# A two-block transformer layer on one core: expert rows fetched one pair ahead, weight buffers split seven and nine, the residual's squares summed later

## The chip, the core and the metric

One NeuronCore of a Trainium2 chip runs the whole program in one launch. Five engines work side by side, each with its own instruction queue: TensorE (PE in the profile; its weight loads are PEld), VectorE (DVE), ScalarE (ACT), GpSimd (POOL) and SyncE (SP, which here only issues transfers). The metric is the device time of one execution in microseconds (us); lower is better.

## The reference

The input is 512 tokens of width 2048, in float32. The first block is a mixer (half convolution, half a recurrent scan) with a residual, `h = x + mixed @ w_out`, followed by a mixture of experts: `v = rms_norm(h)`, a router picks a group of 8 experts by the group logits, then the best 2 of the group for every token, and

    hid = silu(xblk @ w_gate[e]) * (xblk @ w_up[e]);  h += gate * (hid @ w_down[e])

for 32 experts with `w_gate`, `w_up` of 2048 x 512 and `w_down` of 512 x 2048. A last RMS norm gives x1. The second block norms x1 again, makes attention, a state-space branch and two gates from projections of it, merges them, and returns `x1 + merged @ w_out`. The two norms in a row need, per token, the sum of the squares of h (for x1 itself, the residual) and a weighted sum of the same squares (for the input of the second block).

## The kernel before, in words

The program has three phases on one instruction stream per engine. A scheduler orders each engine's instructions when the kernel is built, by program order and by the time at which it thinks the operands are ready; on the chip each engine then runs its queue in that order. `issue_after(x)` only tells the scheduler to put the instructions of a block behind x on x's engine.

**Phase A** (lines 168 to 659) is the mixer. Its end is `w_out(1, held)` (lines 250 to 279): for four column blocks of 512 it multiplies, adds the residual, writes the rows of h to a DRAM tensor `dTok` (line 274, POOL's queue), and calls `routed` (lines 703 to 740), which transposes the block into `hT`, adds to the router's logits and sums squares for the first norm. For the first three blocks the logits are made with the 36 router columns as the stationary operand (line 721) and turned at the end (line 729), for the last with tokens as the stationary operand (line 735).

**Phase B** (lines 743 to 1013) is the mixture of experts, worked in 16 pairs of experts; each expert of a pair has 64 rows (slots). Weights come in loads of 1 MiB (line 676, SP's queue), 24 for a pair: 8 gate, 8 up, 8 down. They go round 16 buffers of 8 KB per partition, in two pools: `NW[0]` = 11 on the right side of the SBUF, which exist while phase A still runs and are filled during `w_out(1)` (line 260), and `NW[1]` = 5 on the left, which take over memory of phase A and are filled at the start of phase B (line 993). `slot` (line 685) deals the buffers out in turn; the 8 down loads of the last pair use left buffers only, since the right side is given to the next phase's activations (`last`, line 980).

For a pair p these steps follow one another:

- `first` (line 801) makes a one-hot matrix `oh` from the ranks (line 780, DVE), multiplies it with token numbers, scale and gate (line 784, PE), turns the result into row numbers (line 790, DVE) and fetches the rows of h from `dTok` into the one buffer `xg` by an indirect transfer on POOL's queue (line 791).
- `turned` (line 808) transposes `xg` in 16 matmuls (line 815, PE), scales it (line 816) into the one buffer `xT`, and transposes `oh` (line 820).
- `main` (line 907) multiplies `xT` with gate and up weights (line 916), makes `hid` (lines 921 to 929), multiplies it with the down weights (line 937), and adds the result, spread over the tokens by lines 946 and 947, to `hT` (line 948).

In program order `first` of pair p+1 stands ahead of `main` of pair p, and `turned` of pair p+1 stands inside it, behind the last up matmul (`then`, line 918). After pair 7 (`BREAK`) the order is interrupted: 15 weight loads are put ahead (line 1007), a branch looks whether any expert has more than 64 tokens (`overflow`, line 955), and only then `first` and `turned` of pair 8 follow, with nothing of a pair beside them. Before the first fetch `xg` is filled with zeros (line 768, POOL), so that slots without a token hold finite numbers.

**Phase C** (lines 1188 to 1464) is the second block. At its start 16 squares are made from `hT` (line 1212, ACT), and two sums over them are kept at once: `acc[1]`, weighted, on DVE (line 1215), and `acc[0]`, plain, on POOL (line 1216). Each ends in a matmul with ones and a reciprocal square root (lines 1219 to 1223): R for the projections, R1 for the residual, which is used in the very last stage only (line 1460). Beside this the dense projections begin: each load of weights is rounded by ACT (line 47), the rest is taken by DVE (line 48), and three matmuls per step use them (lines 111 to 113). hT is written to the DRAM tensor `dX` (line 1230). Much later comes the gated stage (lines 1429 to 1439), two dense products per step with two activation functions.

Of the kernel before, what the change touches and what calls it, by code (L numbers as in the profile page):

```python
# [15 lines left out]
NW = (11, 5)  # L16
# [82 lines left out]
def weights(k, src, kts, m, key="w", eng=None):  # L99

    nc = k.nc
    raw = k.wraw.tile([128, kts, m], F32, name=key + "raw")
    k.wload = nc.sync.dma_start(raw, src)
    wh = k.wspl.tile([128, kts, m], F32R, name=key + "h")
    wl = k.wspl.tile([128, kts, m], F32R, name=key + "l")
    split(nc, raw, wh, wl, eng)
    return wh, wl

# [59 lines left out]
def phase_a(k):  # L168
# [81 lines left out]
    def w_out(half, held=None):  # L250

        mh, ml = mix[half]
        for i, n in enumerate((3, 0, 1, 2) if half else range(4)):
            ns = slice(n * 512, (n + 1) * 512)
            ps = held if half and n == 3 else [k.psd.tile([128, T], F32, name="pd") for _ in range(4)]
            for j in range(8):
                wh, wl = weights(k, a["w_out"][half, n, j], 1, 512, eng=None if half else nc.gpsimd)
                if half and (j == 7 or i and j % 2):
                    with tc.issue_after(k.wload.ins):
                        k.ahead(1, NW[0])  # L260
                for t in range(4):
                    ts = slice(t * 128, (t + 1) * 128)
                    mm3(nc, ps[t], mh[:, j, ts], ml[:, j, ts], wh[:, 0], wl[:, 0], j == 0 and ps is not held,
                        j == 7 and (half == 1 or n < 3))
# [382 lines left out]
    k.dH = tc.dram_tile([T, D], F32, name="dTok")  # L647
    k.rw = rm.tile([128, KT, 36], F32, name="rw")
    k.lgT = tmp.tile([128, T], F32, name="sg")
# [53 lines left out]
def routed(k, psr, tmp, xs, n, i):  # L703

# [10 lines left out]
    if i < 3:  # L718
        pl = psr.tile([128, T], F32, name="pr")
        for j in range(4):  # L720
            nc.tensor.matmul(pl[0:36], k.rw[:, 4 * n + j], k.hT[:, 4 * n + j], start=j == 0, stop=j == 3)
        if i == 0:
            nc.scalar.activation(k.lgT[0:36], pl[0:36], AF.Copy)
        else:
            nc.vector.tensor_add(k.lgT[0:36], k.lgT[0:36], pl[0:36])
        if i == 2:
            pl = psr.tile([128, 4, 36], F32, name="pr")
            for t in range(4):
                nc.tensor.transpose(pl[:, t], k.lgT[0:36, t * 128:(t + 1) * 128], k.ident[0:36, 0:36])
            nc.scalar.activation(k.lg, pl, AF.Copy)  # L730
    else:
        pl = psr.tile([128, 4, 36], F32, name="pr")
        for t in range(4):
            for j in range(4):
                nc.tensor.matmul(pl[:, t], k.hT[:, 4 * n + j, t * 128:(t + 1) * 128], k.rw[:, 4 * n + j],
                                 start=j == 0, stop=j == 3)
        nc.vector.tensor_add(k.lg, k.lg, pl)
# [5 lines left out]
def phase_b(k, upto):  # L743
# [24 lines left out]
    nc.gpsimd.memset(xg, 0.0)  # L768
# [138 lines left out]
    def main(xT, info, oht, es, load=k.take, then=None, last=None):  # L907
        nq = slice(0, 64 * len(es))
        pgu = [ps0.tile([128, 512], F32, name=n) for n in ("pgate", "pup")]
        for j0 in range(0, KT, 4):  # L910
            for wi, which in enumerate(("gate", "up")):
                ws = [load(e, which, j0 // 4) for e in es]
                for j in range(4):
                    for i, w in enumerate(ws):
                        q = slice(i * 64, (i + 1) * 64)
                        nc.tensor.matmul(pgu[wi][q], xT[:, j0 + j, q], w[:, j * 512:(j + 1) * 512],  # L916
                                         start=j0 + j == 0, stop=j0 + j == KT - 1)
        if then is not None:
            then()
# [60 lines left out]
    def last():  # L980

        k.bctx.close()
        k.uctx = ExitStack()
        up = k.uctx.enter_context(tc.tile_pool(name="u2", bufs=1, side=RIGHT))
# [8 lines left out]
    k.ahead(NW[1])  # L993
    fr = {}
    prep(0)
# [3 lines left out]

    for p in range(16):  # L1000
        soon = p < 15 and p != BREAK
        if soon:
            ahead_of(p + 1)
        main(*fr.pop(p), (2 * p, 2 * p + 1), k.take, (lambda: prep(p + 1)) if soon else None,
             last if p == 15 and upto != "b" else None)
        if p == BREAK:
# [3 lines left out]
            prep(p + 1)  # L1010
# [177 lines left out]
def phase_c(k, out):  # L1188
    nc, tc, a = k.nc, k.tc, k.a
    ctx = ExitStack()  # L1190
    k.wraw = ctx.enter_context(tc.tile_pool(name="wraw2", bufs=4, side=LEFT))
# [8 lines left out]
    R = c.tile([128, T], F32, name="R")  # L1200

# [6 lines left out]
    with tc.tile_pool(name="nrm", bufs=2, side=LEFT) as np_:  # L1208
        acc = [np_.tile([128, T], F32, name="acc%d" % i, bufs=1) for i in range(2)]
        for f in range(KT):  # L1210
            sq = np_.tile([128, T], F32, name="nsq", bufs=4) if f else acc[0]
            nc.scalar.activation(sq, k.hT[:, f], AF.Square)
            g = col(k, "gg", f)
            if f:
                nc.vector.scalar_tensor_tensor(acc[1], sq, g, acc[1], op0=OP.mult, op1=OP.add)
                nc.gpsimd.tensor_add(acc[0], acc[0], sq)
            else:
                nc.vector.tensor_scalar(acc[1], sq, g, None, op0=OP.mult)
        for x, r, e in ((acc[1], R, 1e-12), (acc[0], R1, 1e-6)):
            pr = psr.tile([128, T], F32, name="pr")  # L1220
            nc.tensor.matmul(pr, k.ones, x, start=True, stop=True)
            nc.vector.tensor_scalar(x, pr, 1.0 / D, e, op0=OP.mult, op1=OP.add)
            rsqrt(k, tmp, x, [128, T], r)
# [202 lines left out]

    yp = ctx2.enter_context(tc.tile_pool(name="ysp", bufs=1, side=RIGHT))
# [13 lines left out]

    wp = ctx2.enter_context(tc.tile_pool(name="mg2", bufs=1, side=LEFT))
# [135 lines left out]
```

## Time and profile before

| what | value |
|---|---|
| median of 3 runs | 3401.13 us (3394.83 to 3404.06) |
| the profiled execution's own time | 3402.26 us |
| its span, first to last instruction | 3400.6 us |
| mean granted TensorE clock | 0.963 of full speed |
| busy: PE, PEld, DVE, ACT, POOL | 93%, 63%, 49%, 31%, 16% |
| share of the chain that ended last | PE 46%, DMA 4%, POOL 2%, DVE 1% |

Times inside the execution are counted from the first instruction. Phase B's expert pairs take from about 1032 to 2041 us. In the rows further down, `out<-in` are the kernel's names, x is a count, a number in brackets is the idle time of the engine just before the row, with what ended it, and a name with two forms of a matmul's size (128*64) gives rows and columns of the array that it uses.

### The profile page before, as it was taken

Reading aid. Unit: us, or ns where it says so; the run is one execution under the profiler, and the core shown is the slowest. Engines: PE = TensorE matmul, PEld = TensorE weight load, DVE = VectorE, ACT = ScalarE, POOL = GpSimd, SP = SyncE. Lnnn points to the kernel's source line nnn. Section 1 sums busy time; section 2 is a strip of 40 time slices with the busy share of each in tenths; the row PEclk is TensorE's granted clock in tenths of the full one; section 3 lists DMA queues with packets and bytes.
Section 4 is the critical chain, followed back from the end, with each engine's and each line's share of the span. In section 5 each row is a group of like instructions: output and inputs, shape, how many; then the busy total and the mean of one; then the engine's idle time right before and its main releaser. Section 6 shows DMA issues by size and latency. Waiting matters only on the chain.

```text
span 3400.6 us, 41331 instructions
## 1 busy us (share of the span) xinstructions
PE 3171.8 (93%) x15156; PEld 2156.7 (63%) x15157; DVE 1658.1 (49%) x3072; ACT 1052.2 (31%) x1793; POOL 546.0 (16%) x581
## 2 busy tenths in 40 slices
PE   8999998779989899898999898999999999999999
PEld 6777666547664333333333346778777878888887
DVE  6666667993332222232223238445799443344433
ACT  6464564344330000000000024363322242353322
POOL 3052254543210000000000005372000100000000
PEclk9999999789999999899999998999999999999999
DMA  4445444767668999998999965435332653334343
GB/s 149 129 122 139 125 121 123 139 131 181 219 239 352 420 420 414 406 407 349 419 420 411 404 249 167 143 144 166 134 106 104 203 183 118 124 130 137 133 146 118
DMA packets 352495, 743.47 MB, mean 219 GB/s; under 512 B 110688, under 2 KB 176608, under 8 KB 302112
## 3 DMA queue, kind: packets, MB, share of 16 engines
q1 hardware_dynamic: 272576, 650.24, 52.1%
q10 hardware_dynamic: 70624, 60.52, 7.2%
q0 software_dynamic: 9088, 30.03, 2.7%
q8 instruction: 121, 1.98, 0.2%
q14 instruction: 86, 0.70, 0.1%
HBM read 674.96 MB, written 73.01 MB: 220 GB/s over the span
## 4 chain that ended last, share of the span: by engine, by line
PE 46%; DMA 4%; POOL 2%; DVE 1%; issue 1%; ACT 0%; ACTq 0%; SPq 0%; DVEq 0%; POOLq 0%
PE pd L113 10%; PE pd L111 10%; PE pd L112 10%; PE pgate L916 3%; PE py L937 3%; PE pup L916 2%; DMA xg<-dTok,ix 1%; DMA w<-expert_w_gate_dram 1%; PE pb L946 1%; PE pb L947 1%; PE pb L815 1%; PE pr L1345 1%; POOL cn L1115 1%; PE ps L1296 0%; POOL cm L1114 0%
## 5 line engine op out<-in xcount | busy, mean ns | idle before, releaser
L48 DVE TENSOR_TENSOR wl<-wraw,wh 128x512 fp32r<-128x512 f32 x636 | 478.0, 754 | 496.0 <-ACT wh L47 487.1
L47 ACT ACTIVATE wh<-wraw 128x512 fp32r<-128x512 f32 x668 | 418.0, 628 | 834.0 <-PE pd L112 677.7
L113 PE MATMUL pd<-u2h,wl 128*128 128x512 f32 x1088 | 437.7, 402 | 10.2 <-DVE wl L48 10.1
L111 PE MATMUL pd<-u2h,wh 128*128 128x512 f32 x1088 | 439.4, 404 | 6.4 <-ACT wh L47 6.4
L112 PE MATMUL pd<-u2l,wh 128*128 128x512 f32 x1088 | 436.6, 401 | 0.0
L113 PE MATMUL pd<-uh,wl 128*128 128x512 f32 x688 | 282.6, 411 | 42.8 <-DVE wl L48 42.8
L916 PE MATMUL pgate<-w,xT 128*64 128x512 f32 x1024 | 305.6, 615 | 15.7 <-DMA w<-expert_w_gate_dram 15.0
L916 PE MATMUL pup<-w,xT 128*64 128x512 f32 x1024 | 293.5, 595 | 0.0
L111 PE MATMUL pd<-uh,wh 128*128 128x512 f32 x688 | 278.7, 406 | 12.0 <-ACT uh L220 7.2
L112 PE MATMUL pd<-ul,wh 128*128 128x512 f32 x688 | 278.1, 404 | 5.0 <-DVE ul L221 5.0
L113 PEld LDWEIGHTS pd<-u2h,wl 128*128 128x128 f32 x1088 | 206.5, 190 | 63.7 <-DVE wl L48 14.0
L309 POOL TENSOR_TENSOR cv<-cv,tap 128x512 f32<-128x512 f32 x150 | 227.6, 1517 | 105.1 <-ACT tap L308 92.4
L111 PEld LDWEIGHTS pd<-u2h,wh 128*128 128x128 f32 x1088 | 206.9, 190 | 56.7 <-ACT wh L47 9.0
L937 PE MATMUL py<-w,hidT 128*64 128x512 f32 x1024 | 236.0, 599 | 2.9 <-ACT hidT L929 2.9
L112 PEld LDWEIGHTS pd<-u2l,wh 128*128 128x128 f32 x1088 | 206.9, 190 | 47.8 <-issue 1.1
L948 DVE TENSOR_TENSOR hT<-hT,pb 128x512 f32<-128x512 f32 x256 | 159.2, 681 | 148.9 <-PE pb L947 148.9
L941 DVE SCALAR_TENSOR_TENSOR yl<-py,info,yh 128x512 fp32r<-128x512 f32 x64 | 48.0, 750 | 311.1 <-ACT yh L940 311.1
L916 PEld LDWEIGHTS pgate<-w,xT 128*64 128x64 f32 x1024 | 87.5, 142 | 170.0 <-issue 157.4
L113 PEld LDWEIGHTS pd<-uh,wl 128*128 128x128 f32 x688 | 134.0, 195 | 82.8 <-DVE wl L48 53.7
L916 PEld LDWEIGHTS pup<-w,xT 128*64 128x64 f32 x1024 | 87.0, 137 | 135.8 <-issue 133.6
L791 POOL DMA_INDIRECT xg<-dTok,ix x16 | 16.1, 1007 | 918.7 <-DVE info L798 908.3
L937 PEld LDWEIGHTS py<-w,hidT 128*64 128x64 f32 x1024 | 71.9, 137 | 143.8 <-issue 133.9
(566 smaller groups left out, 5054.8 us busy)
## 6 DMA issues: line engine op xcount, KB each, us to landing
w<-expert_w_gate_dram SPq DMA_DIRECT2D x128, 1024.0 KB, 14.7
w<-expert_w_up_dram SPq DMA_DIRECT2D x128, 1024.0 KB, 16.0
w<-expert_w_down_dram SPq DMA_DIRECT2D x128, 1024.0 KB, 14.0
wraw<-w_out_dram SPq DMA_DIRECT2D x128, 256.0 KB, 2.7
wraw<-w_rkv_dram SPq DMA_DIRECT2D x96, 256.0 KB, 3.0
wraw<-w_conv_dram SPq DMA_DIRECT2D x64, 256.0 KB, 3.5
wraw<-w_ga_dram SPq DMA_DIRECT2D x64, 256.0 KB, 2.6
wraw<-w_gs_dram SPq DMA_DIRECT2D x64, 256.0 KB, 2.6
```

The lines of the kernel that those rows point to most:

```text
L47: nc.scalar.activation(h, x, AF.Copy)
L48: (eng or nc.vector).tensor_sub(l, x, h)
L111: nc.tensor.matmul(ps, ah, bh, start=first, stop=False)
L112: nc.tensor.matmul(ps, ah, bl, start=False, stop=False)
L113: nc.tensor.matmul(ps, al, bh, start=False, stop=last)
L309: nc.gpsimd.tensor_add(cv[p], cv[p], pr)
L815: nc.tensor.transpose(ps[:, j, 0:m], xg[0:m, (j0 + j) * 128:(j0 + j + 1) * 128], k.ident[0:m, 0:m])
L916: nc.tensor.matmul(pgu[wi][q], xT[:, j0 + j, q], w[:, j * 512:(j + 1) * 512], start=j0 + j == 0, stop=j0 + j == KT - 1)
L937: nc.tensor.matmul(py[q], hidT[:, j, q], w[:, j * 512:(j + 1) * 512], start=j == 0, stop=j == 3)
L941: nc.vector.scalar_tensor_tensor(yl[nq], py[nq], info[nq, 0:1], yh[nq], op0=OP.mult, op1=OP.subtract)
L946: nc.tensor.matmul(ps, yh[nq, fs], og, start=True, stop=False)
L948: nc.vector.tensor_add(hT[:, f], hT[:, f], ps)
```

## The change

- `NW` becomes (7, 9). In `w_out(1)` fewer expert loads are put ahead: one in the first column block and two in each of the others, seven in all.
- `routed` makes the logits of all four blocks with tokens as the stationary operand.
- `xg` is filled by a transfer of 128 rows of x on POOL's queue in place of the zeros.
- In `main`, what `then` holds is ordered behind the last up matmul on PE. It now holds `turned` of pair p+1 and then `first` of pair p+2, so that the rows of pair p+2 are fetched as soon as the transposes of pair p+1 have read `xg`. At the break pair 8 is fetched and turned as before, then pair 9 fetched.
- At the start of phase C only the weighted sum is made. The plain sum moves behind the gated stage: 16 tiles of `dX` are loaded back on ACT's queue, squared by ACT and added by POOL, then normed to R1.
- Some tiles without use (`pad`, `fill`, an early `xr`) move addresses and hold no instruction.

```diff
-NW = (11, 5)
+NW = (7, 9)
...
+def pad(k, ctx, side, n):
+
+    p = ctx.enter_context(k.tc.tile_pool(name="pad", bufs=1, side=side))
+    return p.tile([128, n // 4], F32, name="pad")
...
-                if half and (j == 7 or i and j % 2):
+                if half and (j == 7 or i and j == 3):
                     with tc.issue_after(k.wload.ins):
                         k.ahead(1, NW[0])
...
+    rm.tile([128, 512], F32, name="xr", bufs=4)
     k.rw = rm.tile([128, KT, 36], F32, name="rw")
-    k.lgT = tmp.tile([128, T], F32, name="sg")
...
-    if i < 3:
-        pl = psr.tile([128, T], F32, name="pr")
+    pl = psr.tile([128, 4, 36], F32, name="pr")
+    for t in range(4):
         for j in range(4):
-            nc.tensor.matmul(pl[0:36], k.rw[:, 4 * n + j], k.hT[:, 4 * n + j], start=j == 0, stop=j == 3)
...
+            nc.tensor.matmul(pl[:, t], k.hT[:, 4 * n + j, t * 128:(t + 1) * 128], k.rw[:, 4 * n + j], start=j == 0,
+                             stop=j == 3)
+    if i:
+        nc.vector.tensor_add(k.lg, k.lg, pl)
     else:
...
+        nc.vector.tensor_copy(k.lg, pl)
...
-    nc.gpsimd.memset(xg, 0.0)
+    nc.gpsimd.dma_start(xg, a["x"][0:128])
...
-                        nc.tensor.matmul(pgu[wi][q], xT[:, j0 + j, q], w[:, j * 512:(j + 1) * 512],
+                        up = nc.tensor.matmul(pgu[wi][q], xT[:, j0 + j, q], w[:, j * 512:(j + 1) * 512],
                                          start=j0 + j == 0, stop=j0 + j == KT - 1)
         if then is not None:
-            then()
+            with tc.issue_after(up.ins):
+                then()
...
+        pad(k, k.uctx, RIGHT, 480)
...
-    k.ahead(NW[1])
-    fr = {}
-    prep(0)
...
+    def prepare(p):
+
+        prep(p)
+        if p < 15 and p != BREAK:
+            ahead_of(p + 1)
+
+    k.ahead(NW[1])
+    fr = {}
+    prepare(0)
     for p in range(16):
-        soon = p < 15 and p != BREAK
-        if soon:
-            ahead_of(p + 1)
-        main(*fr.pop(p), (2 * p, 2 * p + 1), k.take, (lambda: prep(p + 1)) if soon else None,
+        main(*fr.pop(p), (2 * p, 2 * p + 1), k.take, (lambda: prepare(p + 1)) if p < 15 and p != BREAK else None,
              last if p == 15 and upto != "b" else None)
         if p == BREAK:
             k.ahead(sum(NW), sum(NW) - 1)
             overflow()
             ahead_of(p + 1)
-            prep(p + 1)
+            prepare(p + 1)
...
+    pad(k, ctx, LEFT, 128)
...
+    c.tile([128, 48], F32, name="fill")
...
-        acc = [np_.tile([128, T], F32, name="acc%d" % i, bufs=1) for i in range(2)]
+    with tc.tile_pool(name="nrm", bufs=1, side=LEFT) as np_:
+        acc = np_.tile([128, T], F32, name="acc")
         for f in range(KT):
...
-                nc.vector.scalar_tensor_tensor(acc[1], sq, g, acc[1], op0=OP.mult, op1=OP.add)
-                nc.gpsimd.tensor_add(acc[0], acc[0], sq)
+                nc.vector.scalar_tensor_tensor(acc, sq, g, acc, op0=OP.mult, op1=OP.add)
...
+        token_norm(acc, R, 1e-12)
...
+    pad(k, ctx2, RIGHT, 480)
...
     gctx.close()
 
+    with tc.tile_pool(name="nr1", bufs=2, side=RIGHT) as np_:
+        acc = np_.tile([128, T], F32, name="acc", bufs=1)
+        for f in range(KT):
+            x = np_.tile([128, T], F32, name="x")
+            nc.scalar.dma_start(x, k.dX[f])
+            if f:
+                nc.scalar.activation(x, x, AF.Square)
+                nc.gpsimd.tensor_add(acc, acc, x)
+            else:
+                nc.scalar.activation(acc, x, AF.Square)
+        token_norm(acc, R1, 1e-6)
```

`token_norm` is the body of the old loop over the two sums: a matmul with ones, a scale on DVE and `rsqrt`.

## Rows read from the trace of the kernel before

**Rows 1.** The page's 40 slices of the span (85 us each), GB/s of transfers.

```profile
GB/s 149 129 122 139 125 121 123 139 131 181 219 239 352 420 420 414 406 407 349 419 420 411 404 249 167 143 144 166 134 106 104 203 183 118 124 130 137 133 146 118
```

**Rows 2.** Windows: length, busy PE, PEld, DVE, ACT, POOL (count), clock, DMA share, GB/s.

```profile
983.00:1009.00 26.00, 26.00 (x131) 19.36 (x129) 7.38 (x11) 6.08 (x15) 2.16 (x4) 1.00 0.17 59
1009.00:1036.00 27.00, 12.71 (x69) 9.65 (x69) 13.96 (x52) 3.47 (x5) 4.00 (x3) 0.62 0.55 214
1051.00:1311.00 260.00, 238.91 (x1072) 97.09 (x1068) 69.45 (x117) 18.99 (x29) 3.98 (x4) 0.96 1.01 420
1532.00:1558.00 26.00, 19.68 (x92) 10.71 (x94) 4.22 (x11) 0.60 (x1) 1.99 (x2) 0.77 0.52 197
2041.00:2078.00 37.00, 26.02 (x84) 19.51 (x85) 36.32 (x35) 14.94 (x25) 22.50 (x14) 0.72 0.14 50
2960.00:3048.00 88.00, 88.00 (x386) 72.19 (x386) 39.11 (x57) 53.49 (x71) 0.00 (x0) 1.00 0.38 128
```

**Rows 3.** The tile xg: waits for its fetches (us, times), their time to landing.

```profile
  DMA xg<-dTok,ix: 66.0, 12
...
DMA to landing us min/median/max: 5.0/9.1/10.0
```

**Rows 4.** Timeline of PE in the expert stage: start us, us, instruction, [idle before].

```profile
1188.95 4.41 PE L916 MATMUL pgate<-w,xT 128*64 128x512 f32 x12 [1.36 <-DMA w<-expert_w_gate_dram]
...
1431.30 1.06 PE L784 MATMUL pb<-G,oh 128*128 128x6 f32 x8
...
1442.98 3.65 PE L815 MATMUL pb<-ident,xg 128*128 128x128 f32 x16 [7.06 <-DMA xg<-dTok,ix]
...
1447.41 1.90 PE L916 MATMUL pgate<-w,xT 128*64 128x512 f32 x6
...
1525.33 0.40 PE L947 MATMUL pb<-oht,yl 128*128 128x512 f32 x1
...
1539.76 3.65 PE L815 MATMUL pb<-ident,xg 128*128 128x128 f32 x16 [6.29 <-DMA xg<-dTok,ix]
...
1544.04 3.65 PE L916 MATMUL pgate<-w,xT 128*64 128x512 f32 x14
...
1638.51 3.22 PE L916 MATMUL pgate<-w,xT 128*64 128x512 f32 x13 [1.36 <-DMA w<-expert_w_gate_dram]
...
1699.60 5.08 PE L916 MATMUL pgate<-w,xT 128*64 128x512 f32 x12 [0.68 <-DMA w<-expert_w_gate_dram]
...
1959.99 2.47 PE L916 MATMUL pgate<-w,xT 128*64 128x512 f32 x10
```

**Rows 5.** DMA queues from 1040 to 1500 us: packets, MB, share.

```profile
q0 software_dynamic: 1008, 3.85, 2.1%
```

**Rows 6.** Timeline of SP: the first refills of the expert stage.

```profile
1035.64 12.62 SPq L676 DMA_DIRECT2D w<-expert_w_down_dram  x8
```

**Rows 7.** Timeline of DVE around the start of phase C.

```profile
2033.63 2.07 DVE L990 SCALAR_TENSOR_TENSOR u2l<-hT,vec,u2h 128x512 fp32r<-128x512 f32 x3
...
2042.76 1.77 DVE L1215 SCALAR_TENSOR_TENSOR acc<-nsq,vec,acc 128x512 f32<-128x512 f32 x1
...
2045.05 2.83 DVE L990 SCALAR_TENSOR_TENSOR u2l<-hT,vec,u2h 128x512 fp32r<-128x512 f32 x2
```

**Rows 8.** Timeline of PE at the start of phase C.

```profile
2050.45 0.80 PE L113 MATMUL pd<-u2h,wl 128*128 128x512 f32 x1 [6.44 <-DVE wl L48]
...
2070.26 0.79 PE L113 MATMUL pd<-u2h,wl 128*128 128x512 f32 x1 [2.40 <-DVE wl L48]
```

**Rows 9.** Groups by line, 985 to 1010 us: busy us, mean ns.

```profile
L735 PE MATMUL pr<-rw,hT 128*128 128x36 f32 x32 | 3.7, 276 | 0.0
...
L721 PE MATMUL pr<-hT,rw 128*36 128x512 f32 x8 | 3.6, 596 | 0.0
```

**Rows 10.** DMA issues: KB each, median us to landing.

```profile
xr<-x_dram ACTq DMA_DIRECT2D x16, 256.0 KB, 4.9
...
us<-dX ACTq DMA_DIRECT2D x16, 256.0 KB, 2.7
```

More of the change, by code (lines that the diff above doesn't have):

```diff
@@ L717, in routed @@
             nc.scalar.activation(ht, pt, AF.Copy)
-    if i < 3:
-        pl = psr.tile([128, T], F32, name="pr")
+    pl = psr.tile([128, 4, 36], F32, name="pr")
+    for t in range(4):
         for j in range(4):
-            nc.tensor.matmul(pl[0:36], k.rw[:, 4 * n + j], k.hT[:, 4 * n + j], start=j == 0, stop=j == 3)
[L722 to L730, printed above, removed]
-    else:
[L732 to L737, printed above, removed]
+            nc.tensor.matmul(pl[:, t], k.hT[:, 4 * n + j, t * 128:(t + 1) * 128], k.rw[:, 4 * n + j], start=j == 0,
+                             stop=j == 3)
+    if i:
+        nc.vector.tensor_add(k.lg, k.lg, pl)
+    else:
+        nc.vector.tensor_copy(k.lg, pl)
     for t, x in enumerate(xs):
@@ L1206, in phase_c, with token_norm @@
     u = k.u
-    with tc.tile_pool(name="nrm", bufs=2, side=LEFT) as np_:
-        acc = [np_.tile([128, T], F32, name="acc%d" % i, bufs=1) for i in range(2)]
+    def token_norm(x, r, e):
+        pr = psr.tile([128, T], F32, name="pr")
+        nc.tensor.matmul(pr, k.ones, x, start=True, stop=True)
+        nc.vector.tensor_scalar(x, pr, 1.0 / D, e, op0=OP.mult, op1=OP.add)
+        rsqrt(k, tmp, x, [128, T], r)
+    with tc.tile_pool(name="nrm", bufs=1, side=LEFT) as np_:
+        acc = np_.tile([128, T], F32, name="acc")
         for f in range(KT):
-            sq = np_.tile([128, T], F32, name="nsq", bufs=4) if f else acc[0]
+            sq = np_.tile([128, T], F32, name="nsq", bufs=4)
             nc.scalar.activation(sq, k.hT[:, f], AF.Square)
@@ L1214, in phase_c @@
             if f:
-                nc.vector.scalar_tensor_tensor(acc[1], sq, g, acc[1], op0=OP.mult, op1=OP.add)
-                nc.gpsimd.tensor_add(acc[0], acc[0], sq)
-            else:
[L1218 to L1223, printed above, removed]
+                nc.vector.scalar_tensor_tensor(acc, sq, g, acc, op0=OP.mult, op1=OP.add)
+            else:
+                nc.vector.tensor_scalar(acc, sq, g, None, op0=OP.mult)
+        token_norm(acc, R, 1e-12)
     for i in range(8):
```

## The prediction

> **What bounds the kernel now.** The page's slices come first: in ten of the 40 the transfers run at 404 to 420 GB/s, nowhere else above 352 [rows 1]. That is the expert stage, and the windows inside it say the same: 420 GB/s and a full DMA share over 260 us [rows 2]. A pair needs 24 loads of 1 MiB, 25.17 MB, and its gather, 0.55 MB (3.85 MB on POOL's queue for the seven gathers of 1040 to 1500 us [rows 5]); at 420 GB/s that is 61.2 us. The trace shows that pace where PE waits for weights: two gate matmuls released by a landing weight, of pair 10 and pair 11, start at 1638.51 and 1699.60, 61.1 us apart [rows 4].
>
> The tile xg shows the second limit: 12 times the transposes waited for the gather, 66.0 us in all, and a gather takes 9.1 us to land in the median [rows 3]. The timeline shows why: pair 7's rows are asked for by line 784, which ends at 1432.36, and PE has 3.6 us of pair 6's up matmuls left before it stands at 1435.92, so 7.06 us of the flight lie open [rows 4]. While PE stands, the 16 buffers fill and the transfers pause later. PE then starts a pair later than its weights allow, and each pair adds to that lag. At the two places where pairs cannot overlap, the break and the end, the lag turns into time.
>
> At the start of phase C the windows row from 2041 to 2078 tells another story: DVE 36.32 of 37 us, PE only 84 matmuls at a granted clock of 0.72 (a mix of the levels 1.2 and 2.4 GHz) [rows 2]. The gated stage gives 386 matmuls in 88 us, 0.228 us each, with PE never idle; 84 of them are 19.2 us, so 17.8 of the 37 us are lost.
>
> **The change part by part.** A measurement of this kernel can tell about 0.3%, 10 us, from no change.
>
> *Gather ahead, up to the break.* The wait of 7 us goes; the next thing late is the weights. I count from a matmul that waited for its weights: pair 3's at 1188.95. Four pairs at 61.2 us later, pair 7 could begin at 1433.8; it began at 1447.41 [rows 4]. Gain 13.6 us.
>
> *The same, behind the break.* Pair 11's gate waited for its weights at 1699.60; four pairs later is 1944.4, and pair 15 began at 1959.99 [rows 4]. Gain 15.6 us. PE can keep that pace: the saturated 260 us moved 109 MB, 4.25 pairs, and PE was busy 238.91 us of them, 56 us a pair [rows 2].
>
> *The break itself.* From the last matmul of pair 7 (1525.33) to the first of pair 8 (1544.04) nothing is taken out: branch, one-hot, gather, transposes stay in line. The open gather waited 6.29 us there while the transfers were idle [rows 2, 4]; with PE earlier, the 15 loads put ahead are still in flight, and the gather lands in 9.1 us [rows 3]. Loss 2.8 us (from 0 to 3.7, the longest landing being 10.0). The hole of the transfers here, 197 GB/s over 26 us [rows 2], stays: they wait for pair 8's first matmuls, which move as a whole.
>
> *Seven and nine buffers, the fill of xg.* Four loads, 4.2 MB or 10 us at 420 GB/s, move from `w_out(1)` to the start of phase B, and xg's fill adds 1 MiB, 2.5 us. From 1009 us on that makes nine loads, the fill and a gather: 11.0 MB, 26 us, done at 1035, while the first refill is only issued at 1035.64 [rows 6]; the stretch had 214 GB/s, the one before 59 [rows 2]. So the bytes cost nothing, but pair 0's gather, which landed in 5.0 us, the shortest, now shares the engines: 9.1 us, a loss of 4.1 (from 0, if left buffers are free before 1009 us, to 7, if it lands behind everything) [rows 3]. On POOL's queue the fill stands ahead of the norm's power (line 164), which it can hold up by about an issue; POOL's three instructions of that stretch took 4.00 us, 1.3 each [rows 2], so 0 to 1.3, and I take 0, since the fill waits for the last rows' writes and the power for the last logits, which end at about the same time. In the last pair nine left buffers instead of five hold the eight down loads. PE did not wait for those; but it would at the new pace, so this guards the 15.6 us and adds nothing. SP's queue gets no new order beyond this.
>
> *Order on PE.* Line 784 of the pair after next stands behind the transposes. Behind it wait `hid`'s transposes, one microsecond later, which is its duration [rows 4], at a point where PE is ahead of its weights: 0, bounds -1 and 1 us per pair.
>
> *Router.* 32 narrow matmuls take 3.7 us, the 8 wide ones 3.6 [rows 9]; three blocks change: 0.
>
> *Phase C's start.* POOL's 15 adds go. Beside them a DVE add took 1.77 us and two u2l 2.83 us; without them three u2l took 2.07, 0.69 each [rows 7]. Ahead of the first late weight rest that is (1.77 - 0.69) + (2.83 - 1.38) = 2.5 us of PE's wait of 6.44. The second wait, 2.40 [rows 8], stands behind slow adds alone and goes; of the 9.0 us that remain of the 17.8, lost to the lower clock behind the waits above all, I take a third, 3.0. Gain 7.9 us, from 2.4 to 17.8. The Trainium skill (GPSIMD Engine Reference, section 1, Specifications) says that POOL shares its SBUF interfaces with VectorE, with contention for VectorE instructions that have two SBUF inputs; the rows on DVE agree.
>
> *The gated stage.* Added: 16 reloads issued on ACT's queue, 16 squares, 15 POOL adds, one norm. PE is busy 88.00 of 88 us there, ACT 53.49, DVE 39.11 [rows 2]. At ACT's mean there, 0.75 us an instruction, the squares are 12 us of ACT; the adds slow up to 15 DVE instructions by (1.77 - 0.69) us, 16 us. Both fit, and R1 is used in the last stage only: 0. By the skill's sentence on shared interfaces the adds would cost DVE here what they cost it before; DVE has that time free. What hides it is PE's weights being rounded one load ahead; if that cover goes, the cost is the third rival's. Memory moves (`pad`, `fill`) hold no instruction: 0.
>
> **Sum.** 13.6 + 15.6 - 2.8 - 4.1 + 7.9 = 30.2 us off the profiled execution's 3402.26 us: 3372. That execution stands 1 us above the median, which I leave.
>
> **The rivals.** *The transfers are bound already (the expert stage gives nothing).* For it: 420 GB/s in most windows. Against it: the lag between weights and PE counted above, 14 and 16 us, is idle time of the transfers too, and 197 GB/s at the break. It would hold if the scheduler still puts the row request late, or if PE's order of pairs lets the wait for weights last as long as the gather's. Then only phase C gains: 3402 - 8 = 3394. Beside it stands the Trainium skill (DMA: Bandwidth & Descriptors, section "Issuing engines are not separate DMA queues"): transfers started by any engine run on the same 16 DMA engines, so by that rule an earlier gather moves no byte faster; no byte has to move faster for the sum.
>
> *Everything goes at once.* Left buffers are free early, the break's gather lands as fast as before, phase C loses none of the 17.8: 29.2 + 17.8 = 47 off, 3355.
>
> *Slower: ACT blocks in the gated stage.* ACT runs in order. If each square waits out its reload on ACT, 16 x (landing + 0.75) us stand against 34.5 us that ACT has free [rows 2]. With the 2.7 us that reloads of the same tensor take in a calm stage that is 55, 21 too many; with the 4.9 us of a busier one 90, 56 too many [rows 10]. It beats the gain of 30 from a landing of about 3.3 us and is measurably slower from 3.9; at 4.9 the time is 3372 + 56 = 3428. Against it: two x buffers let a load run beside the square before, and PE holds rounded weights in three buffers.
>
> **How the numbers follow.** The forecast 0.62, with its own range 3358 to 3386 (start loss 0 to 7, phase C 2.4 to 17.8); the bigger gain 0.12; transfers bound already 0.18; the gated stage 0.08, of which some lands near no change. Below 3391 lie the first two and a little of the third: faster 0.76. Same 0.17, slower 0.07. The range runs from the bigger gain, 3353, to the third case with a little of its spread, 3397.
>
> **What would show it.** Right: xg's row of waits falls from 66 us to one gather at the start and one at the break; the gate matmuls of pairs 4 to 7 and 12 to 15 follow each other at about 61 us and wait for weights; pair 15 begins some 20 us sooner against the stage's start; the windows behind 1311 us hold 420 GB/s; no POOL instruction between phase C's start and the state-space weights, DVE adds of 0.7 us and PE waits there of some 4 us. In the gated stage PE stays without waits beside 16 squares. Wrong: pairs that follow at 64 us or more without a gather's wait; a first gate matmul more than 7 us later than before against the router's last matmul; PE idle behind ACT's rounding in the gated stage.

## The result and the profile after

The changed kernel takes 3346.86 us (median of 4 runs, 3343.75 to 3352.43) beside 3400.28 us of the kernel before on the same chip: ratio 0.9848, 95% interval 0.9831 to 0.9865. The profiled execution took 3347.98 us (span 3346.3) against 3402.26. So 54.3 us went (53.4 between the medians), where 30.2 were forecast; the direction was right, the time lies 6 us below the forecast's range of 3353 to 3397.

The page's slices of the kernel after, in GB/s, answer to [rows 1]: the ten slices behind the one at 382 stand at 420 or 421, but for the one with the break (391).

```profile
GB/s 149 129 125 140 119 128 122 133 142 160 195 202 382 420 421 420 420 421 391 420 420 420 421 316 198 130 158 166 126 107 105 203 189 117 157 142 142 131 147 119
```

The tile xg after answers to [rows 3]: two waits are left, 17.3 us, at the start (8.09) and at the break (9.24), and a gather takes 7.3 us at least to land.

```profile
  DMA xg<-dTok,ix: 17.3, 2
...
DMA to landing us min/median/max: 7.3/9.4/10.0
```

Windows of the kernel after (length, busy time and count of PE, PEld, DVE, ACT, POOL, granted clock, DMA share, GB/s): two long stretches of the expert stage, the break, the start of phase C and the gated stage, the last two as long as those of [rows 2].

```profile
1311.00:1500.00 189.00, 179.13 (x757) 68.55 (x756) 48.65 (x79) 13.88 (x21) 1.00 (x1) 1.00 1.01 420
1520.00:1540.00 20.00, 17.84 (x82) 9.16 (x84) 3.84 (x8) 0.60 (x1) 1.00 (x1) 0.81 0.75 303
1560.00:1980.00 420.00, 402.13 (x1778) 159.07 (x1775) 113.61 (x194) 32.95 (x50) 5.98 (x6) 1.00 1.01 420
...
2002.00:2039.00 37.00, 34.30 (x138) 27.11 (x139) 30.05 (x58) 19.83 (x33) 8.87 (x12) 0.95 0.45 147
2902.00:2990.00 88.00, 86.17 (x370) 69.91 (x369) 42.72 (x53) 57.87 (x82) 20.32 (x15) 0.98 0.52 169
```

The first three stretches of the kernel before, the break's a little longer there (1520 to 1546), had 406, 238 and 412 GB/s and a granted clock of 0.93, 0.74 and 0.95:

```profile
1311.00:1500.00 189.00, 172.37 (x760) 73.37 (x760) 50.27 (x82) 13.89 (x21) 1.99 (x2) 0.93 0.99 406
1520.00:1546.00 26.00, 13.68 (x58) 9.38 (x57) 11.03 (x20) 1.28 (x2) 1.00 (x1) 0.74 0.60 238
1560.00:1980.00 420.00, 384.15 (x1709) 158.88 (x1706) 108.12 (x180) 30.93 (x47) 5.98 (x6) 0.95 1.00 412
```

Where the time went, by PE's timeline (stages cut at their first and last matmuls):

| stretch | before | after | gain |
|---|---|---|---|
| end of pair 7's scatter matmuls | 1525.73 | 1504.38 | 21.4 |
| from there to the end of the expert stage | 515.1 | 497.5 | 17.6 |
| from there to the end of the u2 matmuls of phase C | 914.2 | 896.8 | 17.4 |
| gated stage | 87.9 | 92.1 | -4.2 |
| merge stage and `w_out2` | 353.6 | 351.5 | 2.1 |

That is the whole difference. The surprise stands in PE's order, which the scheduler ("the planner" in the expectations below) lays out from the order of the code and its own forecast of when data come. Timeline of PE for one pair (start, us, instruction, idle time ahead), before and then after:

```profile
1378.18 3.65 PE L815 MATMUL pb<-ident,xg 128*128 128x128 f32 x16 [7.34 <-DMA xg<-dTok,ix]
...
1386.56 0.66 PE L927 MATMUL pb<-ident,hid 128*128 128x128 f32 x4
...
1387.63 3.59 PE L916 MATMUL pup<-w,xT 128*64 128x512 f32 x14
...
1393.20 7.04 PE L937 MATMUL py<-w,hidT 128*64 128x512 f32 x32
1400.07 1.45 PE L916 MATMUL pgate<-w,xT 128*64 128x512 f32 x5
...
1412.15 1.94 PE L937 MATMUL py<-w,hidT 128*64 128x512 f32 x8
```

```profile
1411.56 3.65 PE L908 MATMUL pup<-w,xT 128*64 128x512 f32 x14 [1.31 <-DMA w<-expert_w_up_dram]
1415.14 1.97 PE L807 MATMUL pb<-ident,xg 128*128 128x128 f32 x16
1416.94 0.60 PE L812 MATMUL pb<-ident,oh 128*128 128x128 f32 x4
1417.38 0.60 PE L920 MATMUL pb<-ident,hid 128*128 128x128 f32 x4
1418.71 4.50 PE L930 MATMUL py<-w,hidT 128*64 128x512 f32 x18 [0.74 <-ACT hidT L922]
...
1437.76 3.65 PE L930 MATMUL py<-w,hidT 128*64 128x512 f32 x14
1441.34 0.98 PE L940 MATMUL pb<-oht,yl 128*128 128x512 f32 x3
...
1442.71 1.07 PE L908 MATMUL pgate<-w,xT 128*64 128x512 f32 x2
```

Before, gate and up matmuls of the next pair stand among the down matmuls (py) of this one. After, the next pair's transposes come, then all of the downs, then the next pair's gates: PE uses the weights in the order in which SP loads them (gate and up blocks in turn, then the downs). What SP waits for, 1360 to 1480 us (line, us, times, longest), shows what that does. Before:

```profile
SPq L676 <- PE pgate L916: 43.5, 12, 15.4
SPq L676 <- PE py L937: 36.6, 8, 6.1
SPq L676 <- PE pup L916: 23.7, 14, 3.3
```

After:

```profile
SPq L682 <- DMA w<-expert_w_up_dram: 34.3, 16, 2.8
SPq L682 <- DMA w<-expert_w_down_dram: 33.6, 15, 3.3
SPq L682 <- DMA w<-expert_w_gate_dram: 33.5, 16, 2.1
SPq L682 <- PE pup L908: 1.0, 3, 0.3
```

Before, SP waited 103.8 of 120 us for PE to let a buffer go; after, 101.4 us for its own earlier loads and some 3 us for a reader of a buffer. With 420 GB/s throughout, the transfers are now the limit themselves.

The end of pair 7 and the starts of pairs 8 and 15 after the change, which the accounts below use:

```profile
1503.99 0.39 PE L940 MATMUL pb<-oht,yl 128*128 128x512 f32 x1
...
1526.58 3.66 PE L908 MATMUL pgate<-w,xT 128*64 128x512 f32 x13
...
1941.11 1.07 PE L908 MATMUL pgate<-w,xT 128*64 128x512 f32 x2
```

### The profile page after: what moved, and what is told of

Read it like the earlier page. It is cut to its first block, busy times and chain, and to the rows that moved or that the text cites. A ratio compares the mean times of both kernels' runs of the same rounds, so it can differ in the third digit from the quotient of the medians.

```text
span 3346.3 us, 41504 instructions
## 1 busy us (share of the span) xinstructions
PE 3165.2 (95%) x15224; PEld 2156.2 (64%) x15225; DVE 1641.1 (49%) x3073; ACT 1061.2 (32%) x1809; POOL 539.7 (16%) x581
## 5 line engine op out<-in xcount | busy, mean ns | idle before, releaser
L908 PE MATMUL pgate<-w,xT 128*64 128x512 f32 x1024 | 280.8, 596 | 7.9 <-DMA w<-expert_w_gate_dram 7.9
L908 PE MATMUL pup<-w,xT 128*64 128x512 f32 x1024 | 276.0, 594 | 12.9 <-DMA w<-expert_w_up_dram 12.7
L930 PE MATMUL py<-w,hidT 128*64 128x512 f32 x1024 | 260.3, 598 | 9.7 <-ACT hidT L922 9.7
L916 DVE SCALAR_TENSOR_TENSOR hid<-pup,info,sl 128x512 f32<-128x512 f32 x16 | 12.0, 751 | 406.5 <-PE pup L908 406.5
L117 PEld LDWEIGHTS pd<-uh,wh 128*128 128x128 f32 x688 | 134.8, 196 | 42.7 <-ACT uh L226 7.3
```

The costliest lines, as they stand in the source:

```text
L117: nc.tensor.matmul(ps, ah, bh, start=first, stop=False)
L908: up = nc.tensor.matmul(pgu[wi][q], xT[:, j0 + j, q], w[:, j * 512:(j + 1) * 512], start=j0 + j == 0, stop=j0 + j == KT - 1)
L916: nc.vector.scalar_tensor_tensor(hid[nq].rearrange("q j p -> q (j p)"), pgu[1][nq], info[nq, 1:2], sl[nq], op0=OP.mult, op1=OP.mult)
L930: nc.tensor.matmul(py[q], hidT[:, j, q], w[:, j * 512:(j + 1) * 512], start=j == 0, stop=j == 3)
```

## The experiments

Runs 1 to 4, 5 to 8, 9 to 12 and 13 to 15 were each taken together on one chip, beside the kernel before, and the ratios are to it. The table gives, beside the medians, the expert stage by two rows of each trace: the first gate matmul's start and the last scatter (yl) matmul's. What is said of PE's order is read from each run's trace.

| run | median us | ratio to before (95%) | stage, first gate to last scatter |
|---|---|---|---|
| before | 3400.28 | | 1008.4 |
| after | 3346.86 | 0.9848 (0.9831 to 0.9865) | 968.3 |
| 1 gather alone | 3387.16 | 0.9962 (0.9948 to 0.9975) | 998.6 |
| 2 order alone | 3363.72 | 0.9890 (0.9873 to 0.9906) | 969.1 |
| 3 old loop | 3384.31 | 0.9958 (0.9941 to 0.9975) | 1002.7 |
| 4 squares back | 3354.48 | 0.9866 (0.9850 to 0.9883) | 968.5 |
| 5 eleven and five | 3352.37 | 0.9861 (0.9845 to 0.9877) | 970.7 |
| 6 no edge | 3373.47 | 0.9921 (0.9907 to 0.9934) | 993.6 |
| 7 no pads | 3350.52 | 0.9852 (0.9837 to 0.9867) | 969.0 |

The rows behind four of these, out of the views of the gate's and the scatter's line (count, ns, first and last start), in this order: before, after, gather alone, order alone.

```profile
L916 PE MATMUL pgate<-w,xT x1024: 592/592/1116, 1032.0 to 2007.9; 128*64 128x512 f32 x171
...
L947 PE MATMUL pb<-oht,yl x256: 387/393/502, 1075.3 to 2040.4; 128*128 128x512 f32 x128
```

```profile
L908 PE MATMUL pgate<-w,xT x1024: 592/592/1082, 1033.2 to 1968.2; 128*64 128x512 f32 x171
...
L940 PE MATMUL pb<-oht,yl x256: 387/393/504, 1077.5 to 2001.5; 128*128 128x512 f32 x128
```

```profile
L916 PE MATMUL pgate<-w,xT x1024: 592/592/1063, 1030.3 to 1997.2; 128*64 128x512 f32 x171
...
L947 PE MATMUL pb<-oht,yl x256: 387/394/502, 1075.0 to 2028.9; 128*128 128x512 f32 x128
```

```profile
L917 PE MATMUL pgate<-w,xT x1024: 592/592/1114, 1034.3 to 1968.9; 128*64 128x512 f32 x171
...
L948 PE MATMUL pb<-oht,yl x256: 387/393/503, 1075.5 to 2003.4; 128*128 128x512 f32 x128
```

### 1. The gather ahead, alone

The kernel before with the new `prepare` loop, without the order edge.

```diff
-        soon = p < 15 and p != BREAK
-        if soon:
-            ahead_of(p + 1)
-        main(..., (lambda: prep(p + 1)) if soon else None,
+        main(..., (lambda: prepare(p + 1)) if p < 15 and p != BREAK else None,
```

> The kernel before with one part of the change: a pair's gather is issued behind the transposes of the pair ahead of it. Buffers (11 and 5), the squares and the order edge stay as before. Theory ORDER (the planner, which now sees the gathered rows early, puts a pair's down matmuls ahead of the next pair's gate matmuls, so that less work is left behind the last weights): the last scatter matmul of pair 7 comes near 1505 instead of 1525, the expert stage ends near 2005 instead of 2041, and the whole is 3402 less some 35, about 3368. Theory BUFFERS (the stage ends sooner since nine left buffers let the last down loads go out sooner): the last down load still waits for one of five buffers, the stage ends no sooner than 2030 and the whole is about 3390. Theory WAIT (only the 66 us of waits on the gather count, each 5.5 us, and the stream of weights hides half): as I forecast, stage end near 2019, whole near 3380.

The waits on the gather go as in the changed kernel (two are left, 8.7 us), and the stage shortens by 9.8 us only. PE's order is a new mixed one: transposes, four gate blocks of the next pair, then the downs. SP goes on waiting for PE in 1360 to 1480 us:

```profile
SPq L676 <- PE py L937: 46.4, 10, 10.3
SPq L676 <- PE pgate L916: 27.3, 10, 5.8
SPq L676 <- PE pup L916: 26.6, 10, 5.6
```

The median and the stage's end (2029.3) come nearest to BUFFERS; runs 2 and 5, which reach the short stage with five left buffers, take that theory out. ORDER failed in one point: an early gather alone does not bring the order about. WAIT, my forecast, promised 22 us from this and got 10.

### 2. The order, alone

```diff
+        with tc.issue_after(k.down.ins) if len(es) == 2 and es[0] not in (0, 2 * BREAK + 2) else nullcontext():
             for j0 in range(0, KT, 4):
...
-                    nc.tensor.matmul(py[q], ...)
+                    k.down = nc.tensor.matmul(py[q], ...)
```

> The kernel before with nothing but an order edge: the gate and up matmuls of a pair are issued behind the last down matmul of the pair ahead. Gather, buffers and squares stay as before, so the waits on the gather stay. Theory ORDER: pair 7 ends near 1510 instead of 1525, the stage some 25 to 35 us sooner, the whole near 3370 to 3378. Theory WAIT: the waits on the gather stay at about 66 us, the order gives nothing, the whole is 3400 to 3410.

This edge, which is not the one of the changed kernel, alone gives 39.3 of the stage's 40.1 us, with the gather where the code had it and eleven and five buffers. WAIT fell: the time came. But the waits on the gather went too (two left, 13.3 us), since the request now lies some gate blocks ahead of the transposes; so this run shows that the edge is enough, and not how much of its 39.3 us is the order's without those waits. SP waits for its own loads, as in the changed kernel. The whole is lower than ORDER had it, 3363.72.

### 3 and 6. The old loop, and no edge, in the changed kernel

Run 3 puts the loop of before back into the changed kernel. Run 6 takes the edge away:

```diff
-            with tc.issue_after(up.ins):
-                then()
+            then()
```

> The changed kernel with the old place of the gather: one-hot, index and gather are again issued behind the whole of the pair ahead. Nine left buffers, the moved squares and the order edge stay. Theory ORDER: down matmuls are again mixed with the next pair's gate matmuls, the expert stage ends near 2030 to 2040, and only the squares' 12 us remain of the gain: 3380 to 3392. Theory BUFFERS: the stage ends near 2005 and the whole is below 3360.

> The changed kernel without the order edge around the transposes, one-hot and gather of the next pair (the gather stays ahead). Theory ORDER: as in the run with the gather alone, the planner puts the transposes and four gate blocks of the next pair ahead of a pair's down matmuls; SP then waits for PE again, and 15 to 30 us are lost: 3362 to 3377. Rival: the edge is idle, since the gather alone sets the order and the nine buffers do the rest: 3345 to 3352.

The old loop brings the old mix of PE back, twelve waits on the gather with 66.5 us, and a stage of 1002.7 us: nine left buffers and the edge are worth 5.7 us in that order. Without the edge the four gate blocks stand ahead of the downs again, SP waits for PE (py 36.3, pgate 27.6, pup 25.0 of 120 us), and 25.3 us of the stage are lost. Both came as ORDER had them. With this loop, gather ahead and edge have to come together: the edge alone gives 5.7 us, the gather ahead alone 14.8, both 40.1. Of the stage's 40.1 us, 25.3 are thus the order's with the gather already ahead.

### 4. Both sums back at phase C's start

```diff
-        token_norm(acc, R, 1e-12)
+        for x, r, e in ((acc[1], R, 1e-12), (acc[0], R1, 1e-6)):
```

with POOL's adds of before, and no block in the gated stage.

> The changed kernel with both sums of squares at the start of the last phase, as before; all else as changed. If the move of the sums is worth the 15.8 us that the u2 dense stage got shorter less the 4 us that the gated stage got longer, this takes 3347 plus 12, about 3359; the expert stage ends at 2000 all the same. If the u2 stage got shorter for another reason (less left over from the expert stage), 3343 to 3349.

The stage is as long as after (968.5). The u2 matmuls take 908.1 us in place of 896.8 and the gated stage 87.1 in place of 92.1: the move gains 11.3 us and pays 5.0 for it, 6.3 net by the traces (7.6 between the medians, which were not taken together). The first expectation had 12 net, the second none, and the median lies between. Of the 17.4 us that the u2 stage gained, some 6 come from elsewhere. These are single profiles: the u2 stage of the other runs with the sums moved (3, 5 to 8, 10, 13) takes from 893.9 to 902.0 us, so by those the move gains between 6 and 14 us there.

### 5. Eleven right and five left buffers

```diff
-NW = (7, 9)
+NW = (11, 5)
-                if half and (j == 7 or i and j == 3):
+                if half and (j == 7 or i and j % 2):
```

> The changed kernel with eleven right and five left weight buffers again (and the loads ahead of the stage as before). Theory ORDER: the PE order is that of the changed kernel, so nearly all of the gain stays; only the last three down loads wait for a left buffer, which costs 0 to 8 us at the stage's end: 3347 to 3355. Theory BUFFERS: the nine left buffers carry much of the gain: above 3362.

The stage is 2.4 us longer, though the last three down loads had to wait for a left buffer again; BUFFERS falls. Pair 0's transposes wait 5.4 us for their gather in place of 8.1: that is what nine loads ahead of it cost. The median is 5.5 us above the changed kernel's, which was not taken with it. In the profile 5.1 us more stand in the u2 stage (901.9), where PE waited 3.3 us for DVE's part of the first weight in place of 1.2; since runs 7, 10 and 13 with nine left buffers have 902.0, 900.2 and 901.8 us there, that the buffers cost it is not shown.

### 7. Without pads and filling tile

```diff
-        pad(k, k.uctx, RIGHT, 480)
-    pad(k, ctx, LEFT, 128)
-    c.tile([128, 48], F32, name="fill")
-    pad(k, ctx2, RIGHT, 480)
```

> The changed kernel without the three empty pads and the filling tile, which only shift where tiles stand in SBUF. If the matmul pitch of the last stage (0.2264 us after, 0.2286 before) hangs on the place of the tiles, the stage gets some 2 us longer and the whole is 3349 to 3352; if not, 3345 to 3349.

`w_out2` takes 175.9 us without them, 174.3 with them; in every profile taken it is 175.9 or 176.0 without and 174.2 to 174.7 with pads. Tiles that hold nothing are worth 1.6 us there, under 1%; why the place matters was not found out. Run 7's profile has 5.2 us more in the u2 stage too; runs 10 and 13, which have the pads, come within 2 us of that, so it is not shown to be the pads'.

### 8 and 9. The residual's sum in the merge stage

```diff
         split(nc, sa, mh[:, i], ml[:, i])
+        with tc.issue_after(gate.ins):
+            x = parked_load(k.dX[i], i, "us")
+            if i:
+                nc.scalar.activation(x, x, AF.Square)
+                nc.gpsimd.tensor_add(R, R, x)
+            else:
+                nc.scalar.activation(R, x, AF.Square)
+    token_norm(R, R1, 1e-6)
```

Run 8 is this without the edge (`gate` is the step's second sigmoid on ACT).

> The changed kernel with the residual's squares summed one block per step of the merge stage (w_attn, w_ssm) in place of all sixteen beside the gated matmuls; the sum stands in the buffer of the other norm, which nobody reads by then. If the 4 us that the gated stage got longer came from the crowd of loads, squares and POOL adds beside its evictions, the gated stage goes back to 88 us, the merge stage grows by under 1 us and the whole is about 3343. If each POOL add costs the same wherever it stands, 3346 to 3349.

> As the run with the sums in the merge stage, with one edge more: each block's load and square is issued on ACT behind that step's second sigmoid, since without it the planner drew all sixteen forward into the gated stage (POOL adds from 2904 to 2944). If the crowd beside the gated matmuls makes that stage 91.5 to 92.1 us long, it goes back to about 88, the merge stage stays within 1 us of 177.4 and the whole is about 3343. If the gated stage's length comes from elsewhere (place of tiles, the end of the u2 stage), it stays at 91 to 92 and the whole at 3346 to 3348.

Run 8 (3346.49 us, ratio 0.9845, 0.9832 to 0.9859) tested nothing: the sixteen blocks were drawn forward, POOL's adds from 2904.0 to 2943.7, and the gated stage stayed at 91.5. With the edge the adds spread from 2994.8 to 3152.4 and the gated stage has PE without a wait at full clock, 87.1 us; the merge stage takes 178.1 in place of 177.2. So the crowd in the gated stage was what made it longer. Run 9's window:

```profile
2898.00:2986.00 88.00, 88.00 (x390) 72.82 (x389) 37.88 (x56) 52.10 (x69) 0.00 (x0) 1.00 0.39 128
```

From the expert stage's end to the last matmul run 9 takes 1336.0 us; the changed kernel takes 1340.4, 1340.3 and 1339.8 in its three profiles. That is 4 us in one profile, and the other paced runs do not bear it out: from the gated stage's start to the last matmul run 11 takes 441.4 us beside 441.7 of run 10, run 14 441.9 beside 443.1 of run 13, since the merge stage takes 179.6 and 180.1 us there; run 9 has 439.9 beside 443.0 to 443.5 of the changed kernel. The medians, 3348.58 us against 3349.93 of the changed kernel beside it, do not tell it from no gain, and 3343 was expected.

### 10 and 13. The hole at the break

Run 10 lets pair 8's gather and transposes run ahead like any other's:

```diff
-        w1 = k.slot()
+        w1, w2, w3 = (k.slot() for _ in range(3))
-                        main(*turned(*first(re, ge)), (e,), load1)
+                        main(*turned(*first(re, ge, w2), w2, w3.rearrange(...)), (e,), load1)
-        if p < 15 and p != BREAK:
+        if p < 15:
             ahead_of(p + 1)
-            k.ahead(sum(NW), sum(NW) - 1)
+            k.ahead(sum(NW), sum(NW) - 3)
```

with the count read into registers ahead of pair 7. Run 13 adds to it that pair 8's loads behind the branch are issued on ACT:

```diff
-        nc.sync.dma_start(w, a["expert_w_" + which]...)
+        q = nc.scalar if late else nc.sync
+        q.dma_start(w, a["expert_w_" + which]...)
```

> The changed kernel with pair 8's gather and transposes ahead too: the overflow branch between pairs 7 and 8 gets its rows and their transpose in two weight buffers of its own (13 instead of 15 loads stand ahead of it), and the count is read into registers before pair 7. If the hole of transfers at the break (1520 to 1540 at 303 GB/s, worth 5.6 us) comes from PE's chain there (branch, one-hot, 9.2 us of gather, transposes), pair 8 starts near 1512 instead of 1527, the hole shrinks and the whole gains 3 to 6 us: 3341 to 3344. If 13 loads ahead are too few or the branch itself holds SP, the hole stays: 3345 to 3349.

> As the run with pair 8's gather and transposes ahead of the branch, and the eleven loads that follow the thirteen are issued on ACT's queue in place of SP's. If the hole of transfers at the break is SP's (at the end of the branch it waits for all of its loads to land: nine waits from 1508.6 to 1528.0), the transfers stay near 420 GB/s from 1500 to 1560, PE finds its weights, the expert stage ends 4 to 6 us sooner than 2003 and the whole is 3345 to 3348. If the hole comes from the thirteen loads or from PE, the stage ends at 2002 to 2004 and the whole is 3351 to 3354.

In run 10 PE starts pair 8 at 1507.93, 0.45 us behind the branch and 18.7 us sooner than in the changed kernel, and gains nothing: 3353.02 us (ratio 0.9861, 0.9846 to 0.9876; neither expectation had it so high), stage 968.3 us, 309 GB/s from 1520 to 1540. PE had used up the loads ahead by 1529.7 and then stood 10.6 us for a gate load that left at 1529.44. SP's row of the branch's line says why it left so late; first the changed kernel's, then run 10's.

```profile
L956 SPq EVENT_SEMAPHORE  x9: 17/17/17, 1510.2 to 1530.7; - x9
```

```profile
L956 SPq EVENT_SEMAPHORE  x9: 17/17/17, 1508.6 to 1528.0; - x9
```

At the end of the branch SP's queue holds waits on the semaphores of its own loads (eight of the nine), so it goes on only when what it has issued has landed, some 20 us later; its next load goes out at 1530.89, or 1528.10. In run 13 (3348.43 us, ratio 0.9840, 0.9819 to 0.9862) ACT's first loads too leave only at 1530.35, just behind SP's last wait at 1530.3 (what held them the trace does not name); the hole stayed (300 GB/s), and PE waited 11.2 us for the gate load that ACT issued at 1531.72. The stage takes 968.9 us, no less than before this edit; the median lies just above the range of the first expectation and outside that of the second. So PE's chain is ruled out as the cause of the hole in the changed kernel; that SP's wait is the cause is well supported, but the hole was not taken away. In the kernel before both stood there. What SP waited for around the break, before (1500 to 1565) and after (1500 to 1535; line, us, times, longest):

```profile
SPq L676 <- PE pgate L916: 20.4, 6, 13.6
...
SPq L963 <- SPq L963: 12.6, 6, 2.7
```

```profile
SPq L956 <- SPq L956: 21.0, 9, 3.7
```

Before, SP came out of the branch at 1533.6, issued one load and then waited up to 13.6 us for a buffer that pair 8's gate matmuls read; these began at 1544.04. After, they began at 1526.58, ahead of SP's return at 1530.8. The transfers before, in two windows:

```profile
1520.00:1540.00 20.00, 7.68 (x29) 4.74 (x27) 7.57 (x15) 0.69 (x1) 1.00 (x1) 0.75 0.77 309
1540.00:1560.00 20.00, 20.00 (x96) 9.81 (x97) 3.84 (x8) 0.60 (x1) 1.00 (x1) 0.90 0.58 226
```

### 11, 12, 14 and 15. The edits together, beside the changed kernel again

Run 11 joins runs 9 and 10, run 14 joins 9 and 13; 12 and 15 are the changed kernel, taken with them.

> Both of these edits together. If each gains as its theory says, 3337 to 3341; the two stand in stages that have nothing in common, so the gains add up within 1 us.

> The changed kernel as it is, on the same chip as the three variants: 3345 to 3349, as before.

> The same with the squares paced over the merge stage too. If both gain, 3337 to 3342; if the loads on ACT gain nothing, 3344 to 3347 like the run with both edits.

> The changed kernel as it is, on the same chip: 3345 to 3351.

Run 11 takes 3345.41 us (0.9837, 0.9824 to 0.9850) beside 3349.93 (0.9853, 0.9836 to 0.9869) of run 12; run 14 3346.60 (0.9833, 0.9814 to 0.9852) beside 3355.82 (0.9866, 0.9844 to 0.9888) of run 15. Both beat the kernel before; that they beat the changed kernel is not shown, and the gains that the expectations hoped for (3337 to 3342) did not come. The changed kernel itself came out above what was expected of it both times, by 0.9 and 4.8 us. Run 14 fits the second of its expectations, by which the loads on ACT gain nothing. The three profiles of the changed kernel begin pair 0's gates at 1033.2, 1035.9 and 1032.8 us: 3 us come and go ahead of the expert pairs between executions of one kernel.

## Why the prediction was right or wrong

**Gather ahead, to the break (13.6) and behind it (15.6).** These are the terms that failed, and with them the step that priced PE's order at 0, with bounds of -1 and 1 us per pair. I measured the lag at a pair's first gate matmul and took the rest of the pair as given. Pair 7 began at 1447.41 and ended at 1525.73 before, at 1442.71 and 1504.38 after: the start gained 4.7 us, the length 16.6 (78.3 to 61.7). Pair 15 went from 80.8 us (1959.99 to 2040.8) to 60.7 (1941.11 to 2001.84). The rows could have told it: 78 us for a pair in a stage with a pair each 61 to 65 means that two pairs overlap on PE, and SP's waits, which the working did not use, name PE as holder of the buffers. Removing the waits on the gather is worth 10 us with the old buffers (run 1) and 15 with the new (run 6), the edge of run 2, which removes them too, 39; together it is 40, of which 25 come with PE's order on top of the gather ahead (run 6).

Against the stage's start pair 15 began 20.1 us sooner (928.0 to 907.9), as the list of signs had it. That is in part luck: after the change a pair's first gate matmul stands behind all downs of the pair ahead, before it stood in front of them, so the two starts do not compare, and pair 7 began 4.7 us sooner where 13.6 less the start's 4.1 were forecast. The other half of the stage's 40 us, 20.1, is pair 15's own length, for which the working had no term. Its count was also 2.4 us short in each of the two terms: it set a matmul inside pair 3 and pair 11 (their first stand at 1186.55 and 1697.19) against the first of pairs 7 and 15, and would have had 16.0 and 18.0.

**How the order makes time.** What the trace shows is where: before, the last three down loads left at 2019.89; in run 1 at 2007.16, in run 2 at 1980.81, and after, all eight between 1952.33 and 1972.59. With PE in another order than SP, a load waits for a buffer whose reader stands late, others being free; the tail behind the last weights and the stretch before the break grow. That this is the whole mechanism is argued from SP's waits; that an edge on PE's order, with nothing else changed, is enough is shown.

**The break.** Loss 2.8 forecast, 3.9 measured (18.3 to 22.2 us from scatter to gate), with the gather's wait at 9.24. That the hole of the transfers here stays was right in kind and wrong in size: 5.6 us worth of transfers after (20 us at 303 in place of 420), some 14.5 before (20 us at 309 and 20 at 226, from 1520 to 1560). The cause that the forecast named, pair 8's first matmuls, held for the kernel before, where SP waited up to 13.6 us for them behind the branch; after the change SP's waits in the branch stand in its place. These 9 us of transfers are likely part of the 17.6 us gained behind pair 7; no run took them apart.

**The start.** Pair 0's gather landed in 9.4 us, near the 9.1 under load that I took (waits 3.76 to 8.09), but in this profile the chain ahead of it was 2.7 us sooner: pair 0 starts 1.2 us later, not 4.1. Counted from the router's last matmul it starts 3.0 us later (26.0 in place of 23.0; 26.3 and 26.6 in the other two profiles), so the term was near. The nine left buffers, which the forecast had guard its 15.6 us, gave the stage 2.4 us (run 5).

**Phase C's start.** The mechanism held. PE's wait of 6.44 us for DVE [rows 8] is 1.23, the one of 2.40 is gone, the clock is 0.95 in place of 0.72, and 138 matmuls stand in the 37 us that held 84; those 54 are 12.3 us at the 0.228 us that the prediction used. PE's only waits there after the change:

```profile
2003.47 0.50 PE L117 MATMUL pd<-u2h,wh 128*128 128x512 f32 x1 [1.63 <-ACT wh L47]
...
2005.42 0.79 PE L119 MATMUL pd<-u2h,wl 128*128 128x512 f32 x1 [1.23 <-DVE wl L48]
```

The size was off: 11.3 us by run 4, where I had 7.9. The first wait fell by 5.2 us where the working had 2.5; the second went, as forecast; what is left of the 12.3, some 4.7 us, is the clock and small waits, for which it had 3.0. The Trainium skill (GPSIMD Engine Reference, section 1, Specifications) says that POOL shares its SBUF interfaces with VectorE, with contention for VectorE instructions with two SBUF inputs. The trace agrees: without POOL's adds DVE's sums take 0.75 us each, beside them they took 1.60 in the median.

**The gated stage.** I priced it at 0 and named the cover, weights rounded one load ahead. The cover did not hold: PE waited 1.8 us in three places for weights from ACT and DVE, its granted clock was 0.83 from 2938 to 2948, and the stage paid 5.0 us (92.1 in place of 87.1 in runs 4 and 9; 91.7 and 91.6 in the other two profiles of the changed kernel). The rival in which ACT blocks there was right on the place and far off in size: ACT stood 10.7 us for its reloads, which landed in 2.7 us in the median; at that landing the rival had 55 us of ACT's time for reloads and squares.

**The rivals.** "The transfers are bound already" is out: the stage had 40 us. "Everything goes at once" at 3355 is nearest, by luck: left buffers free early and a faster gather at the break, on which it stood, did not come (the start lost 1 to 4 us, the break 3.9).

## What to carry to other kernels

When loads go through a rotating set of buffers, compare the order in which the engine uses them with the order in which they are issued; what the loading queue waits for (its own transfers, or the reader of a buffer) tells which of the two is the limit. A change that moves an early input can change the scheduler's order of everything behind it, so list that order before pricing terms at 0. And look at what a branch does to the queue that has loads in flight, not only to the engine that computes.

## What the runs showed of the hardware

- At the branch SP, with loads in flight, waited 12.6 us before and 21.0 us after for these to land, by wait instructions that stand in its queue; PE crossed in 0.45 us in run 10.
- Sixteen 128x128 transposes take 3.65 us right behind a wait of 7 us and 1.97 us behind busy matmuls (PE's rows at 1378.18 before and 1415.14 after); over 1311 to 1500 us the granted clock was 0.93 with the waits and 1.00 without them.
- The shortest landing of a gather was 5.0 us before, pair 0's, in a stretch of 214 GB/s [rows 2]; the same pair's took 9.4 us after, with the loads of nine left buffers beside it, and the longest was 10.0 us in both kernels.
- Empty tiles that shift others in SBUF change the last stage by 1.6 us.
